# A hybrid decoder step on one core: squares of two norms summed on TensorE, an early table load, and four subtractions moved between engines

## The chip, the core and the metric

The kernel runs on one NeuronCore of a Trainium2 chip. Five engines work beside each other, each on its own queue in a fixed order: TensorE (PE, matmuls, with weight loads shown apart as PEld), VectorE (DVE), ScalarE (ACT), GpSimd (POOL) and SyncE (SP), which here issues all DMA transfers. An instruction that needs another engine's result waits on a semaphore, and everything behind it on its queue waits too. The metric is the device time of one execution in microseconds.

## The reference, cut to what matters

One layer of a causal decoder for 1024 prompt tokens and 8 x 8 sample tokens, with model width 1024 and feed-forward width 2816, all in float32:

```python
def rms_norm(x, g):
    y = xf * lax.rsqrt(jnp.mean(xf * xf, axis=-1, keepdims=True) + EPS)
    return (y * g).astype(x.dtype)

h = rms_norm(x, norm_mix_g)
proj = h @ w_in                       # convolution head group and attention head group
x = x + jnp.concatenate([a, o], axis=-1) @ w_out
h = rms_norm(x, norm_ffn_g)           # the second norm
g_full = jnp.concatenate([ffn_past, h @ w_ffn_gate], axis=1)
g = depthwise_conv_valid(g_full, ffn_conv_w, ffn_conv_b)
x = x + (jax.nn.silu(g) * (h @ w_ffn_up)) @ w_ffn_down
y = rms_norm(x, norm_final_g)         # the last norm
```

## The kernel before

Activations are kept transposed: 128 channels on the partitions, 1088 tokens along the free axis, so x is 8 tiles `x2[0..7]` of 128 x 1088. For precision every operand of a matmul is split into a high part (a copy rounded to fp32r, on ACT) and a low part (the difference, a subtraction on DVE or POOL); each product is three matmuls: high by high, low by high, high by low.

**A norm** needs the sum of squares over channels, that is over the partitions of all eight tiles. ACT squares each tile, DVE adds the eight squares into one tile, and `root` (L199) sums that over its partitions on TensorE: for each piece of up to 128 tokens the tile of squares is loaded as weights and multiplied by a column of ones (L206). Then come two small DVE instructions for mean and epsilon (L210, L213), the reciprocal (L215), the square root on ACT (L216) and one Newton step on DVE (L219 to L221). `spread` (L224) transposes the root back with TensorE (L233), and ACT copies it into a tile `rb` (L235). A square root needs its own function table in ACT; the load of it shows as ACT_TABLE_LOAD.

**The second norm** stands between the output projection and the feed-forward part. The tokens are treated in two halves of 544. `out_half(h)` (L1057) runs the last third of the projection for the eight tiles m: product, residual add (L1066), store to DRAM (`x2d`, L1067), square (L1069) and add (L1073). After half 0 follows half 1, and within half 1 the hook `norm_first` builds the root of half 0: the sum behind block m = 3, the transposes behind m = 6. `first_blocks` scales tiles of half 0 (L1079) and splits them (`split`, L986) into block 11 (tiles 0 to 3), and later block 21 (tiles 4 to 7); the low parts are listed in `made`, so `made[7]` is the last low part of block 21. Then `first_half` (L1102) multiplies the first gate weights with block 11 (tiles px, py), copies them out as `ta` (L1109), calls `between` (the root of half 1, and the blocks 21), multiplies with block 21 into the same px and py, and has `spread_second` spread the second root behind the second step of that product. Behind it the tiles 4 to 7 of half 1 are scaled and split (block 22), the first up weights go through `first_half(up0)`, and the rest of the feed-forward part runs as block products of a Strassen scheme.

**The first up weights.** `weight_raw(w_up, 0)` loads them into two of the tiles with tag WR, of which there are two in all; `weight_parts` (L1005) and `block_tile` (L1013) make the high part on ACT and the low part on POOL. The next weights, of gate pair 1 (`weight_blocks`, L1027), are loaded into the same two tiles once these are read.

**The last norm** follows the down projection. `last_product` (L1482) runs over four chunks of tokens (320, 256, 256, 256) with eight tiles m each: product, add (L1502), square (L1504), add of squares (L1508). The root of a chunk is taken within the next chunk's products; the last chunk's follows at the end, with scaling (L1519) and stores (L1521).

**What sets the order.** The program is traced in the order of the source; a planner then orders the instructions of each engine by that order and by a simulation of when their inputs are there, so an instruction traced later can be placed in a hole that the simulation shows. `tc.issue_after(i)` keeps what is traced under it, on the engine of i, behind i in that engine's queue; it makes no wait between engines.

Of the kernel before, what the change touches and what calls it, by code (L numbers as in the profile page):

```python
# [18 lines left out]
F32 = mybir.dt.float32  # L19
# [5 lines left out]
P = 128  # L25
# [55 lines left out]
def trunk_kernel(tc, xT, w_in, w_out, w_gate, w_up, w_down, par, kc, vc, sa, sf, pmask, smask,  # L81
                 yT, kT, vT, ca, cas, cf):
    nc = tc.nc
    with (
# [114 lines left out]
        def root(sq, div, width):  # L199


            ps = bank(*rbank[0])
            size = sizes(width)
            nt = len(size)
            for i, n in enumerate(size):
                summed[0] = nc.tensor.matmul(ps[:n, i:i + 1], sq[:, i * P:i * P + n], ones, start=True, stop=True).ins  # L206
            v = sp.tile([P, 9], F32, tag="rv", name=nm("rv"), bufs=2)[:, :nt]
            nc.vector.memset(v, 1.0)
            nf = width // P
            nc.vector.tensor_scalar(v[:, 0:nf], ps[:, 0:nf], 1.0 / div, EPS, op0=ALU.mult, op1=ALU.add)  # L210
            if nf < nt:
                n = size[-1]
                nc.vector.tensor_scalar(v[:n, nf:nt], ps[:n, nf:nt], 1.0 / div, EPS, op0=ALU.mult, op1=ALU.add)  # L213
            r = sp.tile([P, 9], F32, tag="rr", name=nm("rr"), bufs=2)[:, :nt]
            nc.vector.reciprocal(r, v)  # L215
            nc.scalar.activation(r, r, AF.Sqrt)  # L216

            t = sp.tile([P, 9], F32, tag="rt", name=nm("rt"), bufs=2)[:, :nt]
            nc.vector.tensor_mul(t, r, r)  # L219
            nc.vector.scalar_tensor_tensor(t, t, -0.5, v, op0=ALU.mult, op1=ALU.mult)  # L220
            rooted[0] = nc.vector.scalar_tensor_tensor(r, t, 1.5, r, op0=ALU.add, op1=ALU.mult).ins  # L221
            return r
# [461 lines left out]
        def weighted(p, hd, u, sc, den, un):  # L684
# [57 lines left out]
            ot = zt("P", "H", HB, "ot", 512)  # L742
            nc.scalar.activation(ot[r0, :], po[r1, :], AF.Copy)
            nc.vector.tensor_add(un[u][r0, :], po[r0, :], ot[r0, :])
# [36 lines left out]

        state = {}

        def finish():
# [98 lines left out]
        prompt_heads(i, 2 * NP)  # L883
        finish()
        out_part(*part)
        for n in PARTS[1:-1]:
# [117 lines left out]

        def weight_parts(x, new):  # L1005
            n = x.shape[-1]
            hi, lo = new
            nc.scalar.activation(hi, x, AF.Copy)
            nc.gpsimd.tensor_sub(lo, x, hi.bitcast(F32))
# [3 lines left out]
        def block_tile(x, zone=False):  # L1013

# [5 lines left out]
            nc.scalar.activation(hi, x, AF.Copy)  # L1020
            nc.gpsimd.tensor_sub(lo, x, hi.bitcast(F32))  # L1021
            return [t.rearrange("p (k c) -> p k c", c=P) for t in (hi, lo)]
# [25 lines left out]
        raw = weight_raw(w_up, 0)  # L1048
        up0 = []
        for i in range(2):  # L1050
            up0 += weight_parts(raw[0][:, i * half:i * half + half], early["up"][2 * i:2 * i + 2])
        up0 += [block_tile(raw[1][:, i * half:i * half + half]) for i in range(2)]

# [3 lines left out]
        def out_half(h, hook):  # L1057
# [4 lines left out]
            for m in range(KT):  # L1062
# [7 lines left out]
                if m == 0:  # L1070
                    acc = s
                else:
                    nc.vector.tensor_add(acc, s, acc)  # L1073
                hook(m)
# [59 lines left out]
        g1, g_shared = first_half(gate0, between, spread_second)  # L1134
        r1 = rs[1]
        for k in range(4):
            scale(1, k + 4, r1)
# [344 lines left out]
        def last_product(t0, n, hook):  # L1482

            acc = None
            for m in range(KT):
# [19 lines left out]
                if m == 0:  # L1505
                    acc = s
                else:
                    added, late = late if m > 1 else None, nc.vector.tensor_add(acc, s, acc).ins  # L1508
                hook(m, last.ins, reduced)
# [129 lines left out]
```

## Time and profile before

| what | value |
|---|---|
| runs of the kernel | 1339.6, 1340.8, 1348.09 us; median 1340.8 |
| profiled execution | 1339.82 us, its span 1338.0 us |
| TensorE busy | 1297.1 us, 97% of the span |
| VectorE busy | 937.9 us, 70% |
| ScalarE busy | 559.8 us, 42% |
| GpSimd busy | 477.0 us, 36% |

The second norm lies at about 580 to 630 us of the span, the last norm from about 1275 us to the end. In a timeline row stand start and length in us, the engine, the line of the kernel, the operation, the tile written and the tiles read, the shapes and a count if rows were joined; the bracket gives the idle time of that engine just before and what ended it. Rows of one engine may overlap a little, since each runs from its first to its last sign of work. SPq is the queue that issues transfers.

### The profile page before, as it was taken

The page shows a single profiled execution, that of the slowest core. Times are in us where ns is not written, and L with a number is a line of the kernel's source. Part 1 is how long each engine was busy: PE and PEld are TensorE (multiplying, and loading weights), DVE is VectorE, ACT ScalarE, POOL GpSimd, SP SyncE. Part 2 cuts the span into 40 slices and gives each one's busy share as a digit, 9 for nine tenths or more (in the row PEclk, how much of TensorE's full clock was granted, in tenths as well). Part 3 has the DMA queues.
Part 4 walks back from the last instruction along what each step waited for, and adds up shares of the span by engine and source line. Part 5 has one row for each costly group of instructions (what it writes and reads, how often), then busy time and mean ns, then how long its engine had stood idle before and what let it go on. Part 6 is the DMA issues. An engine that isn't in the chain of part 4 may idle for free.

```text
span 1338.0 us, 25862 instructions
## 1 busy us (share of the span) xinstructions
PE 1297.1 (97%) x10275; PEld 1245.7 (93%) x10275; DVE 937.9 (70%) x1789; ACT 559.8 (42%) x1128; POOL 477.0 (36%) x375
## 2 busy tenths in 40 slices
PE   7999999999999999988999999999999999999996
PEld 7998988999978887888999999999999999999996
DVE  6379779656666657688976676676766669867656
ACT  6312222256674556445633233332333335334432
POOL 1311211211101103430756456564565534444710
PEclk9999999999999999999999999999999999999999
DMA  8147675955689889262033231332213296352412
GB/s 290 56 128 260 234 275 179 242 163 135 206 249 273 270 261 255 90 219 80 2 122 122 91 109 46 122 122 91 99 56 122 76 337 234 108 178 93 156 40 96
DMA packets 92762, 210.27 MB, mean 157 GB/s; under 512 B 13793, under 2 KB 42721, under 8 KB 92641
## 3 DMA queue, kind: packets, MB, share of 16 engines
q1 hardware_dynamic: 92640, 208.62, 48.1%
q8 instruction: 81, 1.33, 0.4%
q14 instruction: 41, 0.33, 0.1%
HBM read 152.55 MB, written 56.04 MB: 156 GB/s over the span
## 4 chain that ended last, share of the span: by engine, by line
PE 56%; DVE 3%; issue 1%; ACT 0%; DMA 0%; DVEq 0%; ACTq 0%
PE g L918 5%; PE g L919 5%; PE g L916 5%; PE py L918 5%; PE py L916 4%; PE py L919 4%; PE px L916 3%; PE pz L918 3%; PE px L919 3%; PE pz L919 3%; PE pz L916 3%; PE px L918 3%; PE g L1490 1%; PE g L1491 1%; PE g L1492 1%; DVE sq L1073 1%
## 5 line engine op out<-in xcount | busy, mean ns | idle before, releaser
L160 POOL TENSOR_TENSOR wl<-wr,wh 128x1024 fp32r<-128x1024 f32 (+1 forms) x36 | 66.9, 1858 | 320.0 <-PE g L186 279.7
L184 PE MATMUL g<-xh,wh 128*128 128x384 f32 (+1 forms) x472 | 158.3, 335 | 0.6 <-DVE qkv L447 0.6
L186 PE MATMUL g<-xh,wl 128*128 128x384 f32 (+1 forms) x472 | 157.1, 333 | 0.0
L185 PE MATMUL g<-xl,wh 128*128 128x384 f32 (+1 forms) x472 | 156.8, 332 | 0.0
L919 PE MATMUL g<-ux,as 128*128 128x272 f32 x504 | 145.1, 288 | 0.0
L918 PE MATMUL g<-ux,as 128*128 128x272 f32 x504 | 144.8, 287 | 0.0
L916 PE MATMUL g<-ux,as 128*128 128x272 f32 x504 | 144.8, 287 | 0.0
L1021 POOL TENSOR_TENSOR wb<-wr,wb 128x512 fp32r<-128x512 f32 x84 | 122.8, 1474 | 49.6 <-ACT wb L1020 49.6
L1373 POOL TENSOR_TENSOR as<-ar,as 128x640 fp32r<-128x640 f32 (+1 forms) x56 | 91.5, 1646 | 100.8 <-ACT as L1372 89.1
L1020 ACT ACTIVATE wb<-wr 128x512 fp32r<-128x512 f32 x84 | 52.5, 629 | 160.7 <-DVE wr L1037 101.8
L692 ACT ACTIVATE y<-y,m 128x128 f32<-128x128 f32 (+1 forms) x192 | 88.7, 467 | 26.9 <-DVE m L680 16.7
L916 PEld LDWEIGHTS g<-ux,as 128*128 128x128 f32 x504 | 95.0, 189 | 0.0
L919 PEld LDWEIGHTS g<-ux,as 128*128 128x128 f32 x504 | 94.8, 188 | 0.0
L918 PEld LDWEIGHTS g<-ux,as 128*128 128x128 f32 x504 | 94.7, 188 | 0.0
L1243 DVE SCALAR_TENSOR_TENSOR fc<-gb,prm,fc 128x1104 f32<-128x1104 f32 x44 | 83.4, 1914 | 14.8 <-ACT fc L1241 14.5
L1021 POOL TENSOR_TENSOR wa<-wr,wa 128x512 fp32r<-128x512 f32 x42 | 57.6, 1375 | 97.5 <-ACT wa L1020 73.6
L184 PEld LDWEIGHTS g<-xh,wh 128*128 128x128 f32 x472 | 89.4, 189 | 3.0 <-issue 1.6
L186 PEld LDWEIGHTS g<-xh,wl 128*128 128x128 f32 x472 | 89.3, 189 | 2.2 <-issue 2.1
L185 PEld LDWEIGHTS g<-xl,wh 128*128 128x128 f32 x472 | 89.5, 190 | 0.6 <-issue 0.2
L655 DVE CUSTOM_DVE_ANT_0 y<-s,pmk 128x128 f32<-128x128 f32 (+1 forms) x192 | 63.5, 379 | 37.0 <-PE s L651 34.5
L397 DVE SCALAR_TENSOR_TENSOR cacc<-gp,prm,cacc 128x1024 f32<-128x1024 f32 x60 | 86.8, 1447 | 0.0
L1463 DVE TENSOR_TENSOR x<-g,x 128x544 f32<-128x544 f32 x76 | 52.5, 717 | 32.9 <-PE g L919 32.9
(370 smaller groups left out, 4244.1 us busy)
## 6 DMA issues: line engine op xcount, KB each, us to landing
cr<-in_kc SPq DMA_DIRECT2D x24, 768.0 KB, 7.9
cr<-in_vc SPq DMA_DIRECT2D x24, 768.0 KB, 6.8
ux<-ub SPq DMA_DIRECT2D x63, 272.0 KB, 4.4
kk<-dk SPq DMA_DIRECT2D x48, 256.0 KB, 6.8
wr<-in_w_gate SPq DMA_DIRECT2D x22, 512.0 KB, 3.3
wr<-in_w_up SPq DMA_DIRECT2D x22, 512.0 KB, 4.4
wr<-in_w_in SPq DMA_DIRECT2D x20, 512.0 KB, 5.5
ub<-u SPq DMA_DIRECT2D x18, 544.0 KB, 4.0
```

The lines of the kernel that those rows point to most:

```text
L160: lo_eng.tensor_sub(lo, raw, hi.bitcast(F32))
L184: nc.tensor.matmul(ps[c], whi[:, k, :], xh[:, t0:t0 + n], start=(k == 0), stop=False)
L185: nc.tensor.matmul(ps[c], whi[:, k, :], xl[:, t0:t0 + n], start=False, stop=False)
L186: nc.tensor.matmul(ps[c], wlo[:, k, :], xh[:, t0:t0 + n], start=False, stop=(k == nk - 1))
L397: eng.scalar_tensor_tensor(acc[:, :S], gp[:, j:j + S], col(w0 + j), acc[:, :S], op0=ALU.mult, op1=ALU.add)
L692: nc.scalar.activation(y, y, AF.Exp, bias=m[:, 4 * g + i:4 * g + i + 1], scale=-1.0, accum_out=den[:, g, 2 * hd + u, i:i + 1])
L916: nc.tensor.matmul(ps, whi[:, k, :], xh[:, t], start=(start and k == 0), stop=False, skip_group_check=True)
L918: nc.tensor.matmul(ps, whi[:, k, :], xl[:, t], start=False, stop=False, skip_group_check=True)
L919: nc.tensor.matmul(ps, wlo[:, k, :], xh[:, t], start=False, stop=(k == nk - 1), skip_group_check=True)
L1021: nc.gpsimd.tensor_sub(lo, x, hi.bitcast(F32))
L1243: nc.vector.scalar_tensor_tensor(c[:, :W], gb[i][:, t:t + W], col(C_FW + 3 * f + t), c[:, :W], op0=ALU.mult, op1=ALU.add)
L1373: nc.gpsimd.tensor_sub(lo, raw, hi.bitcast(F32))
```

## The change

Three edits. (1) `root` takes a list of tiles and sums them all on TensorE into the same column. In the second norm the squares of m = 6 and 7 of each half are not added by DVE but handed over beside the accumulated one (three terms); in the last norm the square of m = 7 (two terms). (2) Behind the last copy of the attention (`turned_out`) a square root of one column is put on ACT, whose result nobody reads, so the square-root table is loaded there. (3) The low parts of the first up weights are made on DVE instead of POOL, are traced behind the first gate product instead of ahead of the second norm, and stand behind `made[7]` on DVE's queue. The high parts, on ACT, are traced there too.

```diff
@@ root
+            terms = sq if isinstance(sq, list) else [sq]
             for i, n in enumerate(size):
-                summed[0] = nc.tensor.matmul(ps[:n, i:i + 1], sq[:, i * P:i * P + n], ones, start=True, stop=True).ins
+                for j, s in enumerate(terms):
+                    summed[0] = nc.tensor.matmul(ps[:n, i:i + 1], s[:, i * P:i * P + n], ones, start=(j == 0),
+                                                 stop=(j + 1 == len(terms))).ins
@@ weighted
-            nc.scalar.activation(ot[r0, :], po[r1, :], AF.Copy)
+            turned_out[0] = nc.scalar.activation(ot[r0, :], po[r1, :], AF.Copy).ins
@@
         finish()
+        with tc.issue_after(turned_out[0]):
+            nc.scalar.activation(sp.tile([P, 1], F32, name="table"), ones, AF.Sqrt)
         out_part(*part)
@@ weight_parts(x, new, eng), block_tile(x, zone=False, eng=None)
-            nc.gpsimd.tensor_sub(lo, x, hi.bitcast(F32))
+            eng.tensor_sub(lo, x, hi.bitcast(F32))
...
-            nc.gpsimd.tensor_sub(lo, x, hi.bitcast(F32))
+            (eng or nc.gpsimd).tensor_sub(lo, x, hi.bitcast(F32))
@@
         raw = weight_raw(w_up, 0)
-        up0 = []
-        for i in range(2):
-            up0 += weight_parts(raw[0][:, i * half:i * half + half], early["up"][2 * i:2 * i + 2])
-        up0 += [block_tile(raw[1][:, i * half:i * half + half]) for i in range(2)]
@@ out_half
                 if m == 0:
-                    acc = s
+                    acc = [s]
+                elif m < KT - 2:
+                    nc.vector.tensor_add(acc[0], s, acc[0])
                 else:
-                    nc.vector.tensor_add(acc, s, acc)
+                    acc.append(s)
@@
         g1, g_shared = first_half(gate0, between, spread_second)
         r1 = rs[1]
+        up0 = []
+        with tc.issue_after(made[7]):
+            for i in range(2):
+                up0 += weight_parts(raw[0][:, i * half:i * half + half], early["up"][2 * i:2 * i + 2], nc.vector)
+            up0 += [block_tile(raw[1][:, i * half:i * half + half], eng=nc.vector) for i in range(2)]
@@ last_product
                 if m == 0:
-                    acc = s
+                    acc = [s]
+                elif m + 1 < KT:
+                    added, late = late if m > 1 else None, nc.vector.tensor_add(acc[0], s, acc[0]).ins
                 else:
-                    added, late = late if m > 1 else None, nc.vector.tensor_add(acc, s, acc).ins
+                    acc.append(s)
```

More of the change, by code (lines that the diff above doesn't have):

```diff
@@ L782, in trunk_kernel @@
         state = {}
+        turned_out = [None]
         def finish():
@@ L1003, in weight_raw, with weight_parts @@
             return raw
-        def weight_parts(x, new):
+        def weight_parts(x, new, eng):
             n = x.shape[-1]
@@ L1008, in weight_parts, with block_tile @@
             nc.scalar.activation(hi, x, AF.Copy)
-            nc.gpsimd.tensor_sub(lo, x, hi.bitcast(F32))
+            eng.tensor_sub(lo, x, hi.bitcast(F32))
             hi, lo = [t.rearrange("p (k c) -> p k c", c=P) for t in (hi, lo)]
             return [(hi[:, i:i + 4], lo[:, i:i + 4]) for i in range(0, n // P, 4)]
-        def block_tile(x, zone=False):
+        def block_tile(x, zone=False, eng=None):
             if zone:
```

## The prediction

> **What bounds the kernel now.** I read first the page (busy times), then the table of windows, to find where TensorE is not full, then the engines' timelines in those windows.
>
> ```profile
> span 1338.0 us, 25862 instructions
> PE 1297.1 (97%) x10275; PEld 1245.7 (93%) x10275; DVE 937.9 (70%) x1789; ACT 559.8 (42%) x1128; POOL 477.0 (36%) x375
> 590.00:600.00 10.00, 10.00 (x81) 9.87 (x79) 10.00 (x11) 6.19 (x11) 7.94 (x7) 1.00 0.77 271
> 600.00:610.00 10.00, 8.29 (x64) 7.75 (x63) 9.84 (x21) 6.25 (x12) 2.73 (x2) 1.00 0.76 269
> 610.00:620.00 10.00, 7.69 (x58) 7.21 (x58) 10.00 (x19) 5.23 (x9) 0.00 (x0) 1.00 0.10 36
> 620.00:630.00 10.00, 8.00 (x62) 7.79 (x63) 5.81 (x13) 4.74 (x11) 0.00 (x0) 1.00 0.00 1
> 1300.00:1320.00 20.00, 20.00 (x170) 20.00 (x169) 15.66 (x47) 7.10 (x20) 1.45 (x2) 1.00 0.33 113
> 1320.00:1338.00 18.00, 7.43 (x61) 6.96 (x59) 11.21 (x30) 3.75 (x11) 1.45 (x2) 0.82 0.35 118
> ```
>
> In the window rows the columns are stretch, length, then busy time and count of PE, PEld, DVE, ACT and POOL, the granted clock, DMA share and GB/s. TensorE (PE) is busy 97% of the span, so only stretches in which it isn't full can give time, and every instruction added to a full stretch costs its whole length. Of what the change touches, PE has holes in 600 to 630 (the second norm), where VectorE (DVE) is the full engine (10.00 of 10 in 590 to 600 and 610 to 620), and after 1320. In 1300 to 1320, the last norm's other chunks, PE is full. Where PE waits in the second norm, and for whom:
>
> ```profile
> 601.74 1.18 PE L206 MATMUL g<-ones,sq 128*128 128x1 f32 x10 [1.66 <-DVE sq L1073]
> 602.85 0.39 PE L916 MATMUL g<-mh,wh 128*128 128x272 f32 x1
> ...
> 610.67 0.40 PE L934 MATMUL px<-b11h,wa 128*128 128x272 f32 x1 [0.73 <-ACT b11h L988]
> ...
> 612.58 0.39 PE L936 MATMUL px<-b11l,wa 128*128 128x272 f32 x1 [1.39 <-DVE b11l L989]
> ...
> 614.19 1.10 PE L206 MATMUL g<-ones,sq 128*128 128x1 f32 x10
> 615.22 0.39 PE L936 MATMUL px<-b11l,wa 128*128 128x272 f32 x1
> ...
> 622.00 0.39 PE L934 MATMUL px<-b21h,wa 128*128 128x272 f32 x1 [2.25 <-ACT ta L1109]
> ```
>
> Four waits, 1.66 + 0.73 + 1.39 + 2.25 = 6.03 us, end at these starts (idle time in brackets). From 600.08 (601.74 less 1.66), where PE reaches the first half's sum, to 622.00, where the lower blocks' product starts, 21.92 us pass; 15.89 of them are PE work. The window row from 620 shows no further hole, so what moves the start at 622.00 moves the end of the kernel.
>
> **Second norm: squares of m = 6 and 7 on TensorE.** Each half loses two adds on DVE and gets two more column sums over five pieces. Price of the adds:
>
> ```profile
> 579.61 1.89 DVE L979 TENSOR_TENSOR wl<-wr,wh 128x512 fp32r<-128x512 f32 x3
> ...
> 596.04 1.71 DVE L1073 TENSOR_TENSOR sq<-sq,sq 128x544 f32<-128x544 f32 x1
> 598.31 1.18 DVE L1073 TENSOR_TENSOR sq<-sq,sq 128x544 f32<-128x544 f32 x1
> 600.04 1.55 DVE L1073 TENSOR_TENSOR sq<-sq,sq 128x544 f32<-128x544 f32 x1
> ...
> 613.13 0.73 DVE L1073 TENSOR_TENSOR sq<-sq,sq 128x544 f32<-128x544 f32 x1
> ...
> 619.92 0.77 DVE L1079 SCALAR_TENSOR_TENSOR x<-x,prm,rb 128x544 f32<-128x544 f32 x1
> ...
> 621.51 0.72 DVE L989 TENSOR_TENSOR b21l<-x,b21h 128x544 fp32r<-128x544 f32 x1
> ```
>
> First half: the adds of m = 6 and 7 start at 598.31 and 600.04; both go. What the sum waits for then is the add of m = 5 (596.04, itself stretched from 0.73 to 1.71) and the two squares, all in hand before PE arrives at 600.08. The 1.66 us wait is gone, and nothing takes its place.
>
> Price of the sums: one column sum in fp32 is two instructions, so a half's five pieces were 10. They took 602.85 - 601.74 = 1.11 us and 615.22 - 614.19 = 1.03 us: 0.105 us apiece. A half now has 30, so 20 x 0.105 = 2.1 us more PE time each, 4.2 for both. The first sum thus ends at 600.08 + 1.1 + 2.1 = 603.3 instead of 602.85: the exchange costs 0.4 us, not a gain.
>
> [...]
>
> How much of the 4.2 us is covered? By the floor of PE, 600.08 + 15.89 + 4.2 = 620.17, the lower blocks' product could start 1.83 us earlier than now. What holds it is DVE: scaling and splitting eight blocks (first half), full from 610 to 622. Its last scale starts at 619.92, and the high part and the copy on ScalarE (ACT) follow:
>
> ```profile
> 620.78 0.66 ACT L988 ACTIVATE b21h<-x 128x544 fp32r<-128x544 f32 x1 [0.70 <-DVE x L1079]
> 621.34 0.61 ACT L1109 ACTIVATE ta<-px 128x544 f32<-128x544 f32 x1
> ```
>
> PE's wait to 622.00 is for that copy of px, which stands behind the last high part on ACT. On this lane the change takes out the second half's adds of m = 6 and 7. PE's last block of the projection now ends 0.4 later (610.67 - 0.73 + 0.4 = 610.3), and DVE needs it for that block's residual, so what the add of m = 6 leaves free just before is lost in waiting for it. The add at 613.13 lay in a full lane and gives 0.63 us, the pace of such instructions back to back (1.89 / 3, the row of 579.61). So scale, high part and copy come 0.63 earlier and PE restarts at about 621.35. By then PE has its 20.09 us of work done if it waits at most 1.2 us in between, against 4.37 in the last three waits now: it can, since the longer second sum fills the waits for the split blocks. Bounds: 1.83 gained, or 0.6 lost (the splits' waits stay, and the sum comes behind them). I take **-0.65 us**.
>
> **Table.** The square root's table load moves behind the last copy of attention.
>
> ```profile
> 568.56 1.15 ACT L978 ACTIVATE wh<-wr 128x512 fp32r<-128x512 f32 x2
> 574.20 0.63 ACT L978 ACTIVATE wh<-wr 128x512 fp32r<-128x512 f32 x1 [4.48 <-DMA wr<-in_w_out]
> ...
> 605.37 0.18 DVE L215 RECIPROCAL rr<-rv 128x5 f32<-128x5 f32 x1
> ...
> 604.71 1.28 ACT L216 ACT_TABLE_LOAD   x1
> 606.01 0.21 ACT L216 ACTIVATE rr<-rr 128x5 f32<-128x5 f32 x1
> ```
>
> It lands where ACT idles 4.48 us before 574.20, so its 1.28 us and the dummy instruction hide there; were the idle time gone, they would push the high parts of the last projection by 1.5 us. At its old place it delays the root only from 605.55 (reciprocal done) to 606.01, 0.4 us. With the sum 0.4 later the two cancel, and PE reaches the transposes behind three more blocks anyway: **0**.
>
> **Low parts of the first up weights on VectorE.** Four subtractions leave GpSimd (POOL):
>
> ```profile
> 595.87 1.29 POOL L1009 TENSOR_TENSOR wa<-wr,wa 128x512 fp32r<-128x512 f32 x1 [0.97 <-ACT wa L1008]
> ...
> 599.74 2.99 POOL L1021 TENSOR_TENSOR wb<-wr,wb 128x512 fp32r<-128x512 f32 x2 [0.84 <-ACT wb L1020]
> ...
> 626.48 5.66 DVE L1079 SCALAR_TENSOR_TENSOR x<-x,prm,rb 128x544 f32<-128x544 f32 x8 [4.16 <-ACT rb L235]
> ...
> 600.57 0.37 SPq L1002 DMA_DIRECT2D wr<-in_w_gate  x1
> wr<-in_w_gate SPq DMA_DIRECT2D x22, 512.0 KB, 3.3
> ...
> 646.49 0.64 ACT L1020 ACTIVATE wa<-wr 128x512 fp32r<-128x512 f32 x1 [0.28 <-issue]
> ```
>
> The POOL rows (the first, and the last two as one) lie just where DVE's adds are stretched; without them the remaining adds go back to 0.73. On DVE each costs 0.63 (the row of 579.61 has their very shape), 2.5 us together. They queue behind the last low part of block 21 (621.51 now, about 620.9 then), and what stands behind them on DVE are the eight scales that wait for the second root, first at 626.48 after 4.16 idle (625.8 then). 620.9 + 0.6 + 2.5 = 624.0, so they fit with 1.8 us over: cost 0. Without that cover the scales come 2.5 us later, and block 22 is used only after the up half's 96 matmuls, some 12 us on at 0.124 us each (612.58 to 614.19, 13 starts). Their four high parts stay on ACT, which is busy 6.25 and 5.23 us of 10 in the two windows from 600. The raw weights' two buffers are held until 624 instead of 602.7. On SP's queue two loads wait for them: the next gate weights, now issued at 600.57 and soon after, 3.3 us to land; they would land by 630, and are first read on ACT at 646.49: cost 0, as long as the stores of x2 go ahead of them on the queue.
>
> **Last norm: the last square on TensorE.**
>
> ```profile
> 1304.79 0.57 PE L206 MATMUL r<-ones,sq 128*128 128x1 f32 x4
> 1305.21 0.36 PE L1490 MATMUL g<-ah,wh 128*128 128x256 f32 x1
> ...
> 1327.53 0.42 ACT L1504 ACTIVATE sq<-x 128x256 f32<-128x256 f32 x1 [0.49 <-DVE x L1502]
> ...
> 1327.98 0.43 DVE L1508 TENSOR_TENSOR sq<-sq,sq 128x256 f32<-128x256 f32 x1 [0.21 <-ACT sq L1504]
> ...
> 1328.55 0.58 PE L206 MATMUL r<-ones,sq 128*128 128x1 f32 x4 [2.11 <-DVE sq L1508]
> ```
>
> Chunks 0 to 2 have 3, 2 and 2 pieces; the sums double, so 6 + 4 + 4 = 14 more instructions at 0.105 (four now take 1305.21 - 1304.79 = 0.42): +1.47 us in a stretch where PE has no hole (20.00 of 20). The adds they replace had nobody waiting. In the last chunk PE waits 2.11 us to 1328.55 for the add of 1327.98. Now it waits for the square, which ends at 1327.95: with the same hop (1328.55 - 1328.41 = 0.14) the sum starts at 1328.09, 0.46 earlier. Four instructions are new; the accumulated term's first pair may run before the square is there, so 0.21 to 0.42 comes back. Gain 0.04 to 0.25. Together between +1.2 and +1.45; I take **+1.22 us**.
>
> **Sum.** -0.65 + 0 + 0 + 1.22 = +0.57 us. The profiled execution took 1339.82 (span 1338.0), so 1340.4 there; the median of the runs, 1340.8, lies 0.98 above, so **1341.4 us**.
>
> **Rivals.**
> PE's floor decides, all four waits go: -1.83 and +1.2 give -0.6, 1340.2. For it speaks that the longer sums are free to fill holes; against it that DVE is full where PE waits. Chance 0.24.
> The new sums lie beside their neighbours and cost PE nothing: DVE still holds 621.35, -0.65, and the tail keeps only the 0.46: -1.1, 1339.7. PE's load track has gaps (PEld 7.75 of 10 in 600 to 610), but the 0.105 of both sums and of the tail's four speaks against it: 0.03. [...]
> The splits' waits stay and the second sum follows them: +0.6 + 1.22 give 1342.6. The present order, with a sum placed as a filler at 614.19, is what a planner with other times may lose: 0.15.
> Slower, by the low parts: the planner puts them behind the eight scales rather than ahead of them. The scales run from 626.48 for 5.66 us; the third low part, which the up product's first step needs, is then done at 632.14 + 1.89 = 634.0. PE comes to that product 48 matmuls and five transposes after 622.00, at 622.00 + 53 x 0.124 = 628.6. It stands 5.4 us: 1346.8. It decides as soon as the low parts end later than 628.6. For it: the high parts they need have lost their place in ACT's order. Against it: 4.16 us of idle DVE just there. Chance 0.08.
> That the change doesn't do what it says could be only in the table (a second load before the root). It would take back 0.4 us that isn't on the path: no price.
>
> **How the numbers follow.** Forecast 0.50, the rivals 0.24, 0.03, 0.15, 0.08. The forecast's own range with its bounds is 1340.2 to 1342.5. The runs themselves differ: the lower two by 1.2 us, the third by 7. Leaving out the slow rival and giving both sides about 2.5 us for the runs, the range is 1337.8 to 1345. About 1% (13.4 us) is what a measurement of this kernel can tell from no change; all PE holes touched here sum to some 8 us, so faster by that is excluded but for a new order elsewhere, 0.02; slower, a new order that opens holes, 0.03; within, 0.95.
>
> **What would show it.** Right: no wait of PE at the first half's sum, sums of 30 instructions of some 3.1 us, the lower blocks' product starting 20.6 to 21.5 us after PE reaches the first sum; table load near 568; four subtractions on DVE between the last low part of block 21 and the second root's scales; the tail's full stretch 1.47 us longer and its last sum about 0.46 us nearer to the last matmul. Wrong: a PE wait at the first up product, a wait for gate weights before pair 1, x2 stores stuck behind a load, or the column sums cheaper than 0.105 us.

## The result and the profile after

| | before | changed |
|---|---|---|
| median of 9 runs each, taken side by side, us | 1343.18 (1335.91 to 1351.29) | 1351.06 (1349.42 to 1364.06) |
| ratio of the times, 95% interval | | 1.0081 (1.0053 to 1.0108) |
| profiled execution, us | 1339.82 | 1354.96 |
| its span, us | 1338.0 | 1352.8 |

The changed kernel is slower by 0.0081 x 1343.18 = 10.9 us, with an interval of 7 to 14.5 us. I had forecast 1341.4 and a range up to 1345: wrong, and by a multiple of every term of my sum. A second set of runs of the same changed kernel gave 1.0078 (1.0051 to 1.0106). The ratios here and below leave out slow runs; there was one, of 2561.86 us, among the 12 of two_terms_wide_hi.

Line numbers of the changed kernel: column sums L208, second norm's squares L1071 and adds L1075, root and spread L219 and L236, splits L994 and L995, up weights' high and low parts L1014 and L1015 (zone tiles) and L1026 and L1027 (block tiles), table L890, FFN output add L1271, down rounding L1367, last norm's adds L1517.

First, the head of the page and the table of windows of the changed kernel; the columns are those of the prediction's first fence.

```profile
span 1352.8 us, 25958 instructions
PE 1313.5 (97%) x10333; PEld 1260.5 (93%) x10333; DVE 935.9 (69%) x1785; ACT 558.9 (41%) x1129; POOL 466.3 (34%) x371
...
600.00:610.00 10.00, 10.00 (x62) 9.97 (x62) 5.64 (x15) 4.11 (x8) 0.00 (x0) 0.66 0.19 76
610.00:620.00 10.00, 9.29 (x58) 8.74 (x57) 9.75 (x15) 5.80 (x10) 0.00 (x0) 0.75 0.23 86
620.00:630.00 10.00, 9.91 (x71) 9.53 (x71) 4.86 (x14) 2.55 (x5) 0.00 (x0) 0.90 0.00 0
1090.00:1100.00 10.00, 6.89 (x43) 6.71 (x42) 8.61 (x14) 2.60 (x4) 0.00 (x0) 0.83 0.99 360
```

The holes of the second norm are closed: PE is busy 10.00, 9.29 and 9.91 of 10 from 600 on, where it was 8.29, 7.69 and 8.00. But PE, with 58 more recorded matmuls, is 16.4 us busier (1313.5 against 1297.1). One reason stands in the clock's column: 0.66, 0.75 and 0.90, where all three rows of before say 1.00. And a hole has opened 470 us later, at 1090 (6.89 of 10), in a stretch that the change doesn't touch.

PE's timeline in the second norm and at the first up product:

```profile
599.23 3.52 PE L208 MATMUL g<-ones,sq 128*128 128x1 f32 x30
...
603.07 0.43 PE L924 MATMUL g<-ml,wh 128*128 128x272 f32 x1
603.30 0.43 PE L925 MATMUL g<-mh,wl 128*128 128x272 f32 x1
...
608.41 0.29 PE L924 MATMUL g<-ml,wh 128*128 128x272 f32 x1
608.53 0.29 PE L925 MATMUL g<-mh,wl 128*128 128x272 f32 x1
...
613.14 0.50 PE L208 MATMUL g<-ones,sq 128*128 128x1 f32 x4
613.82 3.61 PE L208 MATMUL g<-ones,sq 128*128 128x1 f32 x24 [0.18 <-ACT sq L1071]
...
625.84 0.39 PE L940 MATMUL px<-b21h,wa 128*128 128x272 f32 x1
...
633.38 0.39 PE L940 MATMUL px<-b11h,wa 128*128 128x272 f32 x1 [0.63 <-ACT wa L1014]
```

No wait stands at the first half's sum any more. Behind the sum, matmuls start every 0.23 us (603.07, 603.30) instead of every 0.12 (608.41, 608.53): half clock, and again behind the second sum. In this execution the granted clock was 0.50 from 601.4 to 608.2 and from 615.1 to 621.9, 6.83 us each. The lower blocks' product starts at 625.84, 26.61 us after the first sum, not 20.6 to 21.5.

Where the two executions differ, by stretches of PE's work. "Half clock" is half of the time at which the clock stood at 0.50, an upper bound of what it cost, since it counts waits too. The last column is a second profiled execution of the changed kernel.

| stretch, us | before | of it waits | changed | waits | half clock | changed, again |
|---|---|---|---|---|---|---|
| up to the last attention projection | 579.94 | 22.9 | 577.86 | 21.4 | 3.4 | 580.26 |
| projection and second norm, to block 21's product | 42.06 | 7.5 | 47.99 | 2.2 | 8.5 | 43.43 |
| to the first up product | 6.93 | 0 | 7.53 | 0.6 | 0 | 7.52 |
| to pair 1 | 36.12 | 0 | 36.96 | 0.2 | 0 | 36.95 |
| to the first down product | 420.83 | 0 | 425.70 | 3.8 | 0 | 425.74 |
| to the last norm's stretch | 189.08 | 0 | 192.13 | 0.7 | 1.7 | 191.85 |
| last norm, to the last matmul of the projection | 51.20 | 0 | 52.62 | 0 | 0 | 52.62 |
| to the end | 11.88 | | 11.98 | | | 11.97 |

Two things differ from one execution to the next: the part up to the projection and the half clock in the second norm (8.5 and 3.4 us). All the rest comes back within 0.3 us. Of the largest of these steady rows, +4.9 us before the first down product, 3.1 are one wait; 0.7 are two short waits in pair 1, and 1.1 the waits don't account for. PE's waits by what was waited for (us in total, times, longest), then PE and VectorE (DVE) at the place of the long one in the changed kernel:

```profile
PE g L922 <- DVE u L1271: 3.1, 1, 3.1
...
PE pz L922 <- ACT wb L1026: 0.5, 1, 0.5
```

```profile
1092.65 0.28 PE L925 MATMUL pz<-t4h,wb 128*128 128x272 f32 x1
1096.04 0.36 PE L922 MATMUL g<-ux,as 128*128 128x272 f32 x1 [3.11 <-DVE u L1271]
```

```profile
1090.86 3.26 DVE L1367 TENSOR_TENSOR ux<-ux 128x544 fp32r<-128x544 f32 x5
1094.04 1.22 DVE L1262 TENSOR_TENSOR u<-u,fc 128x480 f32<-128x480 f32 x2
1095.17 0.72 DVE L1271 TENSOR_TENSOR u<-pz,u 128x544 f32<-128x544 f32 x1
```

And the same place before:

```profile
1085.76 0.29 PE L919 MATMUL pz<-t4h,wb 128*128 128x272 f32 x1
1085.88 0.28 PE L916 MATMUL g<-ux,as 128*128 128x272 f32 x1
```

Before, the first down product followed the last product of the up half without a gap. Now it waits until VectorE has emptied that last product (pz), which stands behind five roundings and two adds in VectorE's order. The data of the down product don't come from there; its place in PSUM, where the results of matmuls are written, does: with other banks, in after_slot below, it has no wait. Both programs name the PSUM banks: the last pair of the FFN has px in bank 0, py in 4 and pz in 6 before, and px in 6, py in 2 and pz in 0 after; the first down product takes banks 0 and 1 in both. The rotation of the pairs has moved on by one, and the bank that was long free is now the one emptied last. The two orders part early: px of the first up product has bank 4 before and bank 2 after. Behind the wait the clock is 0.50 from 1096.4 for another 3.41 us, which makes the 0.83 in the window from 1090.

The rest of the changed kernel as VectorE, ScalarE (ACT), GpSimd (POOL) and SP's queue show it:

```profile
566.34 1.28 ACT L890 ACT_TABLE_LOAD   x1
...
631.42 0.62 ACT L1118 ACTIVATE c<-px 128x544 f32<-128x544 f32 x1 [4.37 <-PE px L944]
...
632.70 0.62 ACT L1014 ACTIVATE wa<-wr 128x512 fp32r<-128x512 f32 x1
...
633.77 0.65 ACT L1014 ACTIVATE wa<-wr 128x512 fp32r<-128x512 f32 x1
...
651.77 0.64 ACT L1026 ACTIVATE wa<-wr 128x512 fp32r<-128x512 f32 x1 [1.82 <-issue]
```

```profile
627.63 0.68 DVE L1027 TENSOR_TENSOR wb<-wr,wb 128x512 fp32r<-128x512 f32 x1
...
628.31 0.68 DVE L1027 TENSOR_TENSOR wb<-wr,wb 128x512 fp32r<-128x512 f32 x1
...
633.36 0.69 DVE L1015 TENSOR_TENSOR wa<-wr,wa 128x512 fp32r<-128x512 f32 x1 [4.07 <-ACT wa L1014]
633.97 5.65 DVE L1083 SCALAR_TENSOR_TENSOR x<-x,prm,rb 128x544 f32<-128x544 f32 x8
639.53 0.68 DVE L1015 TENSOR_TENSOR wa<-wr,wa 128x512 fp32r<-128x512 f32 x1
```

```profile
629.06 11.52 SPq L1008 DMA_DIRECT2D wr<-in_w_gate  x2
```

```profile
652.49 9.22 POOL L1027 TENSOR_TENSOR wa<-wr,wa 128x512 fp32r<-128x512 f32 x1 [58.44 <-ACT wa L1026]
```

The table load is where it was meant to be. The first two low parts are where I expected all four, at 627.63 and 628.31. The other two could not be, since their high parts (L1014) stand in ACT's order behind the copies of px and py, for which ACT waits 4.37 us: 632.70 and 633.77. PE stands 0.63 us for the first. The fourth low part comes behind the eight scales. The raw weights' buffers come free that much later, so the next gate weights are issued at 629.06 and some 11 us on, the first high part of the next pair starts at 651.77 instead of 646.49 (18.4 us behind the first up product instead of 17.6), and its low part on GpSimd, beside a busy VectorE, takes 9.22 us. PE waits 0.5 us for a weight (wb) in pair 1.

The last norm:

```profile
1342.57 1.02 PE L208 MATMUL r<-ones,sq 128*128 128x1 f32 x8 [1.49 <-DVE sq L1517]
```

The sum waits 1.49 us, not 2.11, and takes 1.02, not 0.58.

### The profile page after: what moved, and what is told of

Same layout as the page of the kernel before. It is cut to its first block, busy times and chain, and to the rows that moved or that the text cites. A ratio compares the mean times of both kernels' runs of the same rounds, so it can differ in the third digit from the quotient of the medians.

```text
span 1352.8 us, 25958 instructions
## 1 busy us (share of the span) xinstructions
PE 1313.5 (97%) x10333; PEld 1260.5 (93%) x10333; DVE 935.9 (69%) x1785; ACT 558.9 (41%) x1129; POOL 466.3 (34%) x371
## 4 chain that ended last, share of the span: by engine, by line
PE 56%; DVE 3%; ACT 1%; issue 0%; DMA 0%; POOL 0%; DVEq 0%; SPq 0%; ACTq 0%
PE g L922 5%; PE g L924 5%; PE g L925 5%; PE py L925 4%; PE py L924 4%; PE py L922 4%; PE pz L922 3%; PE px L922 3%; PE pz L925 3%; PE pz L924 3%; PE px L925 3%; PE px L924 3%; DVE ux L1367 1%; PE g L1499 1%; PE g L1500 1%; PE g L1501 1%
## 5 line engine op out<-in xcount | busy, mean ns | idle before, releaser
L1027 POOL TENSOR_TENSOR wb<-wr,wb 128x512 fp32r<-128x512 f32 x82 | 118.1, 1451 | 54.1 <-ACT wb L1026 54.1
L1027 POOL TENSOR_TENSOR wa<-wr,wa 128x512 fp32r<-128x512 f32 x42 | 65.5, 1562 | 156.7 <-ACT wa L1026 137.3
L1026 ACT ACTIVATE wb<-wr 128x512 fp32r<-128x512 f32 x84 | 52.5, 628 | 156.8 <-DVE wr L1043 94.7
```

What stands on the lines that cost most here:

```text
L1027: (eng or nc.gpsimd).tensor_sub(lo, x, hi.bitcast(F32))
```

## The experiments

The theories. **A, clock:** a run of 30 one-column sums brings half clock (0.50 for 6.83 us each from 601.4 and from 615.1, where the changed kernel has its two), and that is the loss. **B, bank:** the loss is the wait at the first down product and the half clock behind it, through the moved rotation. **C, low parts:** the high parts that lost their place in ACT's order, with the waits at the first up product and in pair 1. Against all three, **D:** the sums simply cost PE their time and gain nothing.

The 95% interval of a ratio is some 0.004 to 0.006 wide (5 to 8 us), so single microseconds are read from the traces. "Clock lost" below is each run's span times one less its mean granted clock, averaged over the runs of a kernel; with standard errors, before has 12.9 +- 0.4 (25 runs, taken beside sums_only, no_second_sums and wide_ones) and the changed kernel 15.1 +- 0.7 (16 runs, both sets). Beside low_only, hi_early, after_slot and spread_sums before has 13.7 +- 0.5 (30 runs, without one whose mean clock was 0.94), beside the last three 13.1 +- 0.7.

| label | what it is | median us | ratio to before (95%) | clock lost |
|---|---|---|---|---|
| sums_only | before + second norm's sums | 1343.19 | 1.0003 (0.9982 to 1.0024) | 14.2 |
| low_only | before + low parts on VectorE | 1342.62 | 1.0008 (0.9987 to 1.0029) | 11.5 |
| no_second_sums | changed - second norm's sums | 1344.22 | 1.0012 (0.9988 to 1.0036) | 13.2 |
| wide_ones | changed, sums with 64 columns | 1347.48 | 1.0023 (1.0002 to 1.0044) | 11.0 |
| hi_early | low_only, high parts early | 1343.34 | 0.9997 (0.9976 to 1.0018) | 12.6 |
| after_slot | changed, one more pair taken | 1348.94 | 1.0045 (1.0024 to 1.0066) | 14.1 |
| spread_sums | changed, sums in shorter runs | 1347.97 | 1.0053 (1.0024 to 1.0082) | 13.9 |
| after_again | the changed kernel | 1353.93 | 1.0078 (1.0051 to 1.0106) | 14.7 |
| wide_hi | wide sums, early high parts, last norm as before | 1345.09 | 1.0024 (1.0001 to 1.0047) | 12.1 |
| two_terms_wide_hi | the same, one square fewer on PE | 1342.36 | 0.9995 (0.9975 to 1.0015) | 12.5 |

### One part alone, and all but one

sums_only is the kernel before with this alone, and with the loop over the terms in `root`:

```diff
                 if m == 0:
-                    acc = s
+                    acc = [s]
+                elif m < KT - 2:
+                    nc.vector.tensor_add(acc[0], s, acc[0])
                 else:
-                    nc.vector.tensor_add(acc, s, acc)
+                    acc.append(s)
```

> The kernel before with one part of the change: the three-term column sums of the second norm. Clock theory: behind each sum of 30 one-column matmuls (3.1 to 3.5 us) the granted clock falls to 0.5 for 3.4 to 6.8 us, as in the changed kernel (601.4 and 615.1 of its span), which loses 1.7 to 3.4 us each; less the 2 us that the vanished waits are worth, 1.5 to 5 us slower than before, and a mean clock below 0.992. Rival theory (the low parts on VectorE and the late up weights cost the time): no half clock, within 1.5 us of before.

Measured 1.0003: the sums alone cost nothing that shows. Its interval, -2.4 to +3.2 us, leaves room for the lower part of the 1.5 to 5 us expected, no more. So D, the plain price of the sums, isn't the main cause either. Its trace has the long sums and half clock behind the second one, and no wait at the first down product:

```profile
603.26 3.02 PE L208 MATMUL g<-ones,sq 128*128 128x1 f32 x30
...
614.17 3.22 PE L208 MATMUL g<-ones,sq 128*128 128x1 f32 x28
```

From the first sum to block 21's product pass 22.07 us (before 20.26, behind a wait of 1.66), with 3.41 us at half clock. PE's waits in the whole stretch fall from 7.5 to 2.3 us, and the sums take 4.2 us of that back.

no_second_sums is the changed kernel with that edit undone, so the table, the low parts and the last norm stay.

> The changed kernel with the second norm's squares added on VectorE as before; early table, low parts on VectorE and the last norm's two-term sums stay. Clock theory: no half clock between 595 and 625; what is left is the last norm's 1.4 us and, if it belongs to another part, the wait of 3.1 us at the first down product: 1 to 5 us slower than before, mean clock as before. Rival theory (low parts): as slow as the changed kernel, 7 us or more over before.

Measured 1.0012, with no wait at the first down product, but with 6.83 us at half clock from 609.9, where the clock theory had none. The loss is gone within the intervals when the second norm's sums are left out, and when they stand alone: it needs the parts together. The sums' half clock by itself (A, as in sums_only) is not the main cause.

low_only is the kernel before with the low parts alone (all that names `eng` and `made[7]` in the diff); the last norm and the table are as before.

> The kernel before with one part of the change: the first up weights' parts traced behind the first gate product, their low parts on VectorE. Theory (the gains of the parts overlap): TensorE's waits from the projection to block 21's product fall from 7.5 us to 3 to 4, since GpSimd no longer stretches VectorE's adds; against it 1 to 2 us of wait at the first up product, as the high parts come late on ScalarE. Within 2.5 us of before, mean clock as before. Rival (low parts cost the time of the changed kernel): 5 us or more slower.

Measured 1.0008. ACT at the first up product, and PE from the first half's sum to there:

```profile
620.73 0.62 ACT L1114 ACTIVATE c<-py 128x544 f32<-128x544 f32 x1
621.24 0.63 ACT L1012 ACTIVATE wa<-wr 128x512 fp32r<-128x512 f32 x1
```

```profile
593.30 1.10 PE L208 MATMUL g<-ones,sq 128*128 128x1 f32 x10
...
613.28 0.39 PE L938 MATMUL px<-b21h,wa 128*128 128x272 f32 x1 [2.27 <-ACT ta L1109]
...
621.92 0.40 PE L938 MATMUL px<-b11h,wa 128*128 128x272 f32 x1 [1.53 <-ACT wa L1012]
```

PE stands 1.53 us for a high part that is issued late: C's wait is real. It is paid for in the second norm, where PE's waits fall from 7.5 to 5.8 us by this part alone (3 to 4 were expected). The wait at the first half's sum is gone without any square handed to TensorE: the sum starts at 593.30 with no wait ahead of it, and block 21's product 19.98 us later. Before, that took 21.92 us from PE's arrival at the sum. The sums alone bring PE's waits to 2.3 us, both together to 2.2: what the low parts gain the sums gain anyway, while the costs of both are paid.

### Is it the high parts' place?

hi_early is low_only with the four high parts written where they stood before, ahead of the projection, and only the subtractions behind block 21:

```diff
...
+        for x, hi, lo in up_parts:
+            nc.scalar.activation(hi, x, AF.Copy)
...
         with tc.issue_after(made[7]):
-            for i in range(2):
-                up0 += weight_parts(raw[0][:, i * half:i * half + half], early["up"][2 * i:2 * i + 2], nc.vector)
-            up0 += [block_tile(raw[1][:, i * half:i * half + half], eng=nc.vector) for i in range(2)]
+            for x, hi, lo in up_parts:
+                nc.vector.tensor_sub(lo, x, hi.bitcast(F32))
...
```

> As low_only, but the four high parts keep their old place in the trace (on ScalarE, early), and only the low parts stand on VectorE behind block 21. Theory: the gain of low_only without the wait at the first up product, which comes from the high parts: that wait gone, 1 to 4 us faster than before. Rival (the wait comes from the subtractions themselves): the wait at the first up product stays.

Measured 0.9997. The high parts run from 596.86 to 601.45, and the wait at the first up product is gone (0 in the trace), so it was their place. The 1 to 4 us expected don't show: the time is that of low_only and of before within the interval, and a wait of 0.6 to 1.5 us is less than the measurement can see.

### Is it the bank?

after_slot is the changed kernel with one more pair of banks taken just ahead of the first down product, so that this product falls on a pair that is long free:

```diff
+                        if k == 0 and m == 0:
+                            nc.vector.memset(pair("skip")[:, 0:1], 0.0)
```

> The changed kernel, with one pair of PSUM banks taken by an unused tile ahead of the down projection, so that its first product writes banks 6 and 7 and not 0 and 1, which in the changed kernel the last pz of the feed-forward part holds to its end (in the kernel before that pz lies in banks 6 and 7 and px in 0 and 1). Theory (bank order): the wait of 3.1 us at the first down product is gone or below 1 us, with the half clock behind it: 3 to 5 us faster than the changed kernel, 1.0045 to 1.006 of before. Rival (the product waits for the value, not for the bank): the wait stays.

Measured 1.0045 against 1.0081 and 1.0078. The first down product runs as before, with no wait, and the clock is whole:

```profile
1087.81 0.30 PE L922 MATMUL g<-ux,as 128*128 128x272 f32 x1
```

```profile
1087.00:1097.00 10.00, 10.00 (x82) 10.00 (x82) 9.72 (x15) 4.55 (x7) 2.29 (x2) 1.00 1.03 384
```

So 0.0036 x 1343 = 4.8 us go with the wait, with some 4.6 us of uncertainty (4.6 +- 3.8 against both sets of the changed kernel). The trace prices it at 3.11 + 1.71 = 4.8 at most; the rows to the first down product and to the last norm's stretch are 3.2 and 0.9 us shorter than in the changed kernel. B is the largest single cause found, and not the whole.

### Is it the clock?

wide_ones is the changed kernel with 64 columns of ones in the second norm's sums instead of one: as many instructions, all columns but the first of no use. `W` is 64 and `one` a tile of 64 columns of ones there, 1 and `ones` elsewhere:

```diff
-                    summed[0] = nc.tensor.matmul(ps[:n, i:i + 1], s[:, i * P:i * P + n], ones, start=(j == 0),
+                    summed[0] = nc.tensor.matmul(ps[:n, i * W:i * W + W], s[:, i * P:i * P + n], one, start=(j == 0),
```

> The changed kernel, but the second norm's 60 sum instructions stream 64 columns of ones instead of one (64 equal copies of each sum, one is read). Clock theory, if streamed columns are what counts as work: the sums take about the same 3.3 us, the granted clock stays 1.00 behind them, and the time falls by 3.4 to 6.8 us against the changed kernel. If a run of weight loads counts as idle whatever is streamed, or if the half clock comes from the waits beside the sums: two half-clock stretches as before, no gain.

Measured 1.0023. PE, and the window over both sums:

```profile
597.63 3.24 PE L211 MATMUL g<-ones,sq 128*128 128x64 f32 x30
...
608.76 3.46 PE L211 MATMUL g<-ones,sq 128*128 128x64 f32 x28
...
627.16 0.39 PE L944 MATMUL px<-b11h,wa 128*128 128x272 f32 x1 [1.23 <-ACT wa L1018]
```

```profile
600.00:610.00 10.00, 9.35 (x74) 8.62 (x74) 8.62 (x20) 5.35 (x10) 0.00 (x0) 1.00 0.34 130
610.00:620.00 10.00, 9.97 (x78) 9.16 (x78) 9.07 (x17) 5.09 (x10) 0.00 (x0) 1.00 0.03 11
```

The sums are about as long as with one column (3.24 us for 30; 3.02 in sums_only, 3.52 in the changed kernel), and the clock stays at 1.00 behind both. Block 21's product starts 20.91 us after the first sum, inside what I had forecast. In this kernel the rotation of the banks is that of before as well, so it takes away A and B together. Against after_slot, which takes away B alone, the ratio falls from 1.0045 to 1.0023, which is 3.0 us with an uncertainty of 4.0. The clock lost falls from 14.1 +- 0.6 to 11.0 +- 0.8; taken against before's runs of each set it goes from 0.5 above to 1.9 below, 2.4 +- 1.2 us. So A is worth some 2 to 3 us, an estimate. PE's wait at the first up product is longer here, 1.23 us.

bursts and bursts2 put useless column sums between pairs of the kernel before, in the full stretch where nothing waits: 10 to 60 instructions of one column, and of more. The bursts make the kernel longer by themselves, so only the clock behind each burst counts. Each kernel was run once.

```diff
+            for _ in range(n // 2):
+                nc.tensor.matmul(o[:, :w], ident, ones64[:, :w], start=True, stop=True)
```

> The kernel before with useless one-column matmuls put into the full stretch of the feed-forward part, once in the gate and once in the up product of a pair: 10 instructions in pair 2, 20 in pair 3, 30 in 4, 60 in 5, then 64 columns wide 30 in 6 and 60 in 7, and again one column wide 20 in 8 and 30 in 9. Output unchanged. [...] Rival (waits of TensorE halve the clock, bursts don't): no half clock at any of them.

> As bursts, with other sizes, twice each: 60 instructions of 2, 8, 16 and 32 columns (pairs 2, 3, 4, 5), 40 of one column (6 and 7), 24 of one column (8 and 9). [...]

From the kernel bursts: a burst of 30 instructions of one column, one of 60, and one of 60 with 64 columns; then the windows they lie in:

```profile
827.09 3.40 PE L1171 MATMUL pb<-ones,ident 128*128 128x1 f32 x30
851.53 8.85 PE L1171 MATMUL pb<-ones,ident 128*128 128x1 f32 x60
994.83 6.80 PE L1171 MATMUL pb<-ones,ident 128*128 128x64 f32 x60
```

```profile
826.00:846.00 20.00, 20.00 (x164) 20.00 (x164) 13.73 (x16) 6.79 (x9) 8.86 (x11) 1.00 0.17 54
850.00:870.00 20.00, 20.00 (x131) 20.00 (x130) 6.88 (x9) 2.26 (x5) 3.32 (x2) 0.74 0.43 151
994.00:1014.00 20.00, 20.00 (x168) 20.00 (x168) 10.13 (x11) 5.10 (x6) 6.29 (x8) 1.00 0.15 52
```

All bursts of both kernels (where the clock fell within every burst of a size, its length is put as that of as many instructions at full clock):

| instructions | columns | about us at full clock | halved | for, us |
|---|---|---|---|---|
| 10 | 1 | 1.2 | 0 of 2 | |
| 20 | 1 | 2.3 | 1 of 4 | 3.4 |
| 24 | 1 | 2.7 | 1 of 4 | 6.8 |
| 30 | 1 | 3.4 | 1 of 4 | 3.4 |
| 40 | 1 | 4.5 | 4 of 4 | 3.4 or 6.8 |
| 60 | 1 | 6.8 | 2 of 2 | 10.2 and 13.7 |
| 60 | 2, 8, 16 | 6.8 | 6 of 6 | 13.7 |
| 60 | 32 | 6.8 | 2 of 2 | 6.8 |
| 30, 60 | 64 | 3.5, 6.8 | 0 of 4 | |

I had expected half clock behind each burst of 30 and none behind 32 columns; it stood behind one burst of 30 in four, and behind both of 32 columns, for 6.8 us. That long runs of few columns bring half clock is shown: 60 instructions of 1 to 16 columns met it in 8 of 8 bursts though PE was busy 20.00 of 20 there, runs of 64 columns of about the same length in 0 of 4, and a run of the kernel's length (30) in 1 of 4. That is what the two profiles of the changed kernel show, 13.7 us at half clock in one's second norm and 3.4 in the other's. It isn't the only way to it: no_second_sums and hi_early, with sums of 10, had 6.8 us at half clock there as well, beside their waits.

spread_sums cuts the sums of 30 into runs of 12, 12 and 6 between the products:

```diff
+            if 1 <= m <= 3:
+                with tc.issue_after(last):
+                    column_sums(sums_of[0], sq0, HN, ((0, 1), (2, 3), (4,))[m - 1])
```

> The changed kernel, but each 30-instruction sum is cut into runs of 12, 12 and 6, each behind a block or a step of other matmuls. The PSUM banks come in another order too (the last pz in 6 and 7). Clock theory: no half-clock stretch behind the sums, and no wait at the first down product: 1.001 to 1.004 of before, mean clock at or above that of before. Rival (half clock comes from the waits in this stage): half clock as in the changed kernel.

Measured 1.0053. That is above what was expected (1.001 to 1.004), though its trace has what the theory asked for: no half clock in its second norm and no wait at the first down product, whose banks are not those of the last pz. Block 21's product starts 24.42 us after the first sum, since the sum now takes 6.1 us from its first instruction to its last, with products in between. The wait at the second split block is 1.09 us (0.18 in the changed kernel), that at the first up product 1.23 (0.63). From the last attention projection on, the trace is 4.1 us longer than that of before, less than the 7.1 us that the ratio says. Its ten runs lie between 1343.76 and 1358.54, and its mean of clock lost, 13.9 +- 1.6, scatters as widely. So this kernel, without A and B in its trace, isn't shown to be faster than after_slot (1.0045), and why not stays open.

### The changed kernel again, and two repairs

after_again is the changed kernel without an edit.

> The changed kernel once more, beside the two that follow, and for a second trace of it. [...]

Measured 1.0078, with the same 3.11 us at the first down product. That wait belongs to the kernel, not to one execution. Half clock stands behind the second sum alone (3.41 us from 616.4), not behind both.

wide_hi joins wide_ones and hi_early and leaves the last norm's adds on VectorE. two_terms_wide_hi does the same and hands over the square of m = 7 alone:

```diff
-                elif m < KT - 2:
+                elif m < KT - 1:
                     nc.vector.tensor_add(acc[0], s, acc[0])
```

> The changed kernel with everything mended that the runs so far name: 64 columns of ones in the second norm's sums (no half clock, and the banks in the order of before), the high parts of the first up weights traced early (no wait at the first up product), the last norm's squares all added on VectorE (its 1.4 us). Theory: 0.997 to 1.001 of before. Rival (something else still costs): 1.002 or more.

> As wide_hi, with only the square of m = 7 handed over in the second norm: 20 sum instructions a half in place of 30, and one add more on VectorE. Theory (sums and adds are alternatives, and with the low parts off GpSimd the adds no longer hold TensorE up): 2 us less of sums, 0.996 to 1.000 of before. Rival: the wait for the add comes back and takes it all.

Measured 1.0024 and 0.9995. The first misses what was expected (0.997 to 1.001). Its trace is 1.7 us longer than that of before from the last projection to pair 1, 1.6 longer from there to the first down product and 1.2 longer in the down half; behind block 21's product it has 1.7 us of waits, where before has none, and it has 3.41 us at half clock from 581.2, ahead of the sums. The rest stays open. The second is level with before, within what was expected. No kernel tried is faster than the one before by more than its interval.

## Why the prediction was wrong

**Where the 10.9 us are.** Some 4 to 5 are the wait at the first down product and the half clock behind it (after_slot). Some 2 to 3, an estimate, are half clock behind the long sums (after_slot against wide_ones). With both taken away 1.0023 is left, 3.1 us with an uncertainty of 2.8. Late high parts and later gate weights (in the changed kernel 0.60 + 0.84 in the rows to the first up product and to pair 1) and the last norm's 1.42 fit that, but wide_ones' own trace is 6.0 us longer than that of before from the last attention projection on, with 1.69 + 1.19 in those two rows, so the fit shows little. spread_sums has neither in its trace and is at 1.0053, which doesn't fit. That both happen is shown (3.11 us at the first down product in two executions, half clock at 8 of 8 bursts of 60 with 1 to 16 columns); the shares are estimates.

**Second norm, price of the sums: a term was missing.** As forecast there was no wait at the first half's sum, instructions took 0.108 us with the clock whole (3.24 / 30 in wide_ones; forecast 0.105; 3.52 / 30 = 0.117 in the changed kernel, whose clock fell within the sum), and with the clock whole block 21's product started after 20.91 us (wide_ones; forecast 20.6 to 21.5, my estimate of the gain 0.65, there 1.0). In part that is luck. I put the gain down to the adds that go, but low_only keeps all of them and has no wait at the sum either, and 19.98 us: taking GpSimd's subtractions away from beside the adds was enough by itself (as the sums were in sums_only), and this gain of the low parts is not in my sum. Wrong was "0.105 us apiece" as the full price. It was taken from sums of 10 at a granted clock of 1.00, and a run three times as long is not three times as dear: the clock can fall behind it, for 3.41 to 6.83 us each time it did in the changed kernel. I took the clock's column in the windows for a description of before and not for something the change could move.

**"What moves the start at 622.00 moves the end of the kernel": the failed step that cost most.** It holds only as long as the full stretch behind it stays the same, order and places alike. I did allow for "a new order that opens holes" and gave it 0.03, without looking for where an order could matter. The place could be seen before: the first down product needs a pair of banks, and the last product of the up half leaves one so late that only the rotation keeps them apart. That the rotation moved follows from the programs, which part at px of the first up product. What in the new order moved it is not shown.

**Low parts: cost 0, wrong by 0.6 us (1.5 in low_only).** Their own place was right for two of the four. The step that failed is "Their four high parts stay on ACT", priced by ACT's busy share (6.25 and 5.23 us of 10). Free time isn't a place in the order: they were queued behind copies for which ACT waits 4.37 us. My slow rival named just this ("the high parts they need have lost their place in ACT's order") and put its price at 5.4 us; PE stood 0.63. The gate weights, forecast to land by 630, were issued from 629.06 on and cost 0.5 us in pair 1. The x2 stores were not stuck.

**Table: right.** It loads at 566.34, 1.28 us, ahead of two high parts of the last projection. ACT's idle time behind them is shorter for it (2.81 us instead of 4.48), and PE waits for none of it.

**Last norm: right in the full stretch, wrong in the last chunk.** +1.42 us against the 1.47 forecast. Of the 0.04 to 0.25 us to come back, 0.18 came at the end of the sum, but by another way. The sum now waits for the add of m = 6 (L1517), which comes behind m = 7's residual on VectorE, so the wait shrinks by 0.62 (2.11 to 1.49) and not 0.46; and eight instructions instead of four take 0.44 more (1.02 against 0.58). The end of the kernel doesn't show it: 11.98 us after the projection's last matmul, 11.88 before.

**The rivals.** PE's floor (block 21's product 20.09 us after PE's arrival at the sum) was not reached even where the clock was whole (20.91), and the sums were not free. The slow rival had the place of a wait right, at a multiple of its size, and put it down to the low parts instead of the high ones. What cost most was covered only by the 0.03 for a new order, and the clock was on no list.

## What to carry to other kernels

When an edit adds many matmuls of few columns in a row to a full TensorE, price the clock behind them too (60 of one column met 10.2 and 13.7 us at 0.50 here), or give them more columns: 64 cost hardly more time here (3.46 us for 30 instead of 3.40 in the bursts), and the clock stayed at 1.00. When a planner or a rotation assigns buffers, look at each change of stage for the product that takes a bank which another engine empties last (3.11 us of wait here); a change hundreds of microseconds earlier can bring the two together. Two edits that close the same wait gain once and pay twice.

## What the hardware showed that was not expected

A TensorE that was busy without a gap was not always granted its full clock: at 60 instructions of 1 to 16 columns it was half in 8 of 8 bursts and at 60 of 64 columns in none of 2, with PE at 20.00 of 20 in the windows shown. Behind the bursts the time at half clock came in steps of 3.41 us (3.41, 6.83, 10.24, 13.65), and a run of 20 to 30 instructions met it in 3 of 12 cases. Where these steps come from, and why a short run meets half clock only at times, was not shown.

Two instructions of GpSimd took many times as long as their like, beside a long run of VectorE's. The row of 652.49 above is one subtraction of 9.22 us, where the next of its shape (663.20) took 1.29, and VectorE is busy 10.00 of 10 from 652 to 662. Before, the same stretch of VectorE's held a small copy:

```profile
643.68 9.49 POOL L1215 COPY gb<-sft 128x16 f32<-128x16 f32 x1
...
653.15 0.20 POOL L1215 COPY gb<-sft 128x16 f32<-128x16 f32 x1
653.30 2.99 POOL L1021 TENSOR_TENSOR wa<-wr,wa 128x512 fp32r<-128x512 f32 x2
```

The same copy takes 0.20 us (653.15) once VectorE has gone on to other instructions. In both kernels GpSimd came free soon after VectorE turned from additions and subtractions between tiles to those that read a product out of PSUM (gb<-pv,ta, at 653.01 before and 660.47 after): 0.16 and 1.24 us. A busy VectorE alone did not do it: from 653 to 663 of before VectorE was busy 9.91 of 10, and the window counts 11 instructions of GpSimd. So the gate weights that come later lose to this stretch what they did not before: their subtractions came behind it then (653.30, 1.5 us each) and one stands in it now.
